# Row steps of the recurrence's block inverses on GpSimd, two to a place in the program, in a one-core decoder layer

## The chip, the cores and the metric

The kernel runs on one core of one Trainium2 chip. A time is the device time of one execution in microseconds (us). In profile rows PE is TensorE, PEld its weight loads, DVE VectorE, ACT ScalarE, POOL GpSimd and SP the engine that issues most DMAs.

## What is computed

One inference step of a decoder layer for 256 prompt tokens and 8 decoded ones: a SwiGLU FFN, a mixing stage (sliding-window attention beside an RWKV-7 recurrence with 16 heads of 64), and a second SwiGLU FFN. The change lies in the recurrence:

```python
def step(S, inp):
    r_t, lw_t, k_t, v_t, kk_t, a_t = inp
    sa = jnp.einsum('bhij,bhj->bhi', S, -kk_t)
    S = (S * jnp.exp(lw_t)[:, :, None, :] + sa[..., None] * (kk_t * a_t)[:, :, None, :]
         + v_t[..., None] * k_t[:, :, None, :])
    return S, jnp.einsum('bhij,bhj->bhi', S, r_t)
```

The kernel does not run these 256 steps one by one. It cuts the prompt into 4 chunks of 64 tokens. Within a chunk the effect of every token on later ones is a strictly triangular 64x64 matrix for each head, and the chunk needs the inverse of one minus it. That inverse is built from its two 32x32 diagonal blocks and one product that joins them.

## The kernel before, in words

**Stages.** All matmuls are fp32 work done as three products of split operands (`hi` and `lo`). `chunk` loads a piece of a weight of 128x512 into one of 6 buffers `raw` (SP), rounds it to `hi` (ACT, line 123) and subtracts `lo = raw - hi` (DVE, line 58), with 4 buffers each for `hi` and `lo`; `gemm` then issues 12 matmuls of 264 columns on it, into a PSUM tile `acc`. The first FFN ends at about 764 us, the mixing stage at about 1256 us, the second FFN fills the rest.

**The mixing stage** streams the input projection (38 tiles, `win`) and the output projection (three passes, `wout`) through `gemm`. All else is written as generators (`prep`, `chain`, `attend`, `dec_load`, `dec_attend`); after each `chunk` a `tick` moves each of them one `yield` further. `prep` runs for each of 8 pairs of heads, `chain` for each of 4 batches of two pairs. So a `yield` sets how many ticks a chain spans. The scheduler then reorders the instructions of each engine by a timeline of its own, and on the chip each engine works through its list strictly in that order.

**A chain.** `prep` multiplies out the triangular matrices `gm` and stores their diagonal blocks in a scratch tensor `sa` in DRAM. `chain` loads them twice: `X` holds a block on each of 32 partitions, copied four times (128 partitions), `Y` (called `Xt` in the profile) holds a quarter of its columns on each copy, 8 of 32. Then 30 row steps follow: step `s` multiplies (into `st`) and adds. `Y` goes to a second scratch tensor `sb` and comes back with other axes as `TT`; the unit diagonal is added there; `TN` is its transpose on DVE. Behind `TN` come the joining matmuls (`zs`), `kr`, `W`, `PT`, the products `N` and the steps over the 4 chunks (`Z`, `S`).

**Other names.** In `prep`, `wc`, `XD` and `t` are small tiles of the decode path; GpSimd copies to `XD`, then computes `t<-XD`, 16 columns that the matmul with the block matrix in `C` reads (PE's `m<-t,C`). `shc` are the last columns of each projected tile `pj`. `NSTEP` is the number of row steps for one `yield`, `DWAIT` the ticks that a chain waits after its loads, by batch.

Of the kernel before, what the change touches and what calls it, by code (L numbers as in the profile page):

```python
# [10 lines left out]
ALU = mybir.AluOpType  # L11
# [18 lines left out]
NS, NO, NY, NH, NT, NLD = 38, 8, 8, 40, 18, 6  # L30
NWARM = 14
NGM, NKR, NUV, NTT, NBT = 10, 5, 3, 2, 5
NSTEP = 4
DWAIT = (8,8,8,4)
PW = (2, 1, 3, 2, 2)
ALPHA = math.exp(-0.5)
LKV = 26
# [10 lines left out]
def body(tc, I, O):  # L48
    nc = tc.nc
    V, A, G, TE, SP = nc.vector, nc.scalar, nc.gpsimd, nc.tensor, nc.sync  # L50
# [6 lines left out]
    def tt(e, out, a, b, op):  # L57
        return e.tensor_tensor(out=out, in0=a, in1=b, op=op)  # L58
# [11 lines left out]
    def bc(ap, shape):  # L70
        return ap.broadcast_to(list(shape))
# [15 lines left out]
    def spawn(g):  # L87
        tasks.append(g)
        return g

    def pause(n):
        for _ in range(n):
            yield

    with ExitStack() as ctx:
# [7 lines left out]
        def slot(shape=(P, T), dt=F32, tag="s"):  # L103
            return sp.tile(list(shape), dt, tag=tag, bufs={"s": NS, "o": NO, "y": NY}[tag], name=uid(tag))

        def tmp(shape=(P, T), dt=F32):
            pool, n = cur[0]
            return pool.tile(list(shape), dt, tag="t", bufs=n, name=uid("t"))
# [223 lines left out]
        def mixing_body(mx, n2, n3, XD):  # L332
# [3 lines left out]
            def ring(shape, tag, bufs):  # L336
                return mx.tile(list(shape), F32, tag=tag, bufs=bufs, name=uid(tag))
# [6 lines left out]
            ident, bo, cm = C[:, CID:CID + P], C[:, CBO:CBO + P], C[:, CCM:CCM + P]  # L344
# [27 lines left out]
            def shifted(t, d):  # L372
                ps = win(t)
                pj = PJ[t % 3]
                with tc.high_priority():
                    tt(V, pj[:, 1:1 + T], ps[:, :T], rs, ALU.mult)
                G.tensor_copy(shc[:, t, :], pj[:, NP:NP + NB + 1])
                act(d[:, :NP], pj[:, 0:NP], AF.Copy, scale=vc(VMU + t))
                A.copy(d[:, NP:], ss[:, t, :])
                stt(d, pj[:, 1:1 + T], nmu[:, t:t + 1], d, ALU.mult, ALU.add)  # L380
                return d
# [133 lines left out]
            def chain(bt):  # L515
                n = bt.n
                while bt.left:
                    yield
                nr = n * 16
                ng = P // nr  # L520
                if ng == 3:
                    ng = 2
                nj = 32 // ng
                X = ring((ng * nr, 32, 32), "X", 1)
                Y = ring((ng * nr, nj, 32), "Xt", 1)
# [4 lines left out]
                TT = ring((P, n * 4, 64), "TT", NTT)  # L530
                for h in range(2):
                    G.memset(TT[h * 64 + 32:h * 64 + 64, :, 0:32], 0.0)
                yield from pause(DWAIT[bt.i])
                for s in range(1, 31):
                    m, w = -(-s // ng), 31 - s
                    t = ring((ng * nr, m, w), "st", 2)
                    shp = (ng * nr, m, w)
                    tt(V, t, bc(X[:, s:s + 1, s + 1:], shp), bc(Y[:, :m, s:s + 1], shp), ALU.mult)
                    tt(V, Y[:, :m, s + 1:], Y[:, :m, s + 1:], t, ALU.add)
                    if s % NSTEP == 0:  # L540
                        yield
                for g in range(ng):
                    SP.dma_start(scr2[bt.i].rearrange("r (j g t) -> g r j t", g=ng, t=32)[g], Y[g * nr:(g + 1) * nr])
                yield from pause(1)
                for h in range(2):
                    for blk in range(2):
                        x = h * 64 + blk * 32
                        SP.dma_start(TT[x:x + 32, :, blk * 32:blk * 32 + 32],
                                     scr2[bt.i].rearrange("(h b m) (s t) -> h b s m t", h=2, b=2, s=32)[h, blk])
                yield from pause(DWAIT[bt.i])  # L550
                for h in range(2):
                    for blk in range(2):
                        x = h * 64 + blk * 32
                        v = TT[x:x + 32, :, blk * 32:blk * 32 + 32]
                        tt(V, v, v, bc(ident[x:x + 32, x:x + 32].unsqueeze(1), (32, n * 4, 32)), ALU.add)
                TN = ring((P, n * 4, 32), "TN", 1)
                for h in range(2):
                    V.transpose(TN[h * 64:h * 64 + 32], TT[h * 64:h * 64 + 32, :, 0:32])
# [2 lines left out]
                for k in range(n):  # L561
                    for c in range(4):
                        for h in range(2):
                            j = k * 4 + c
# [26 lines left out]
                for k in range(n):  # L591
                    v = wus[k].rearrange("p (c t) -> p c t", c=4)
# [5 lines left out]
                for k in range(n):  # L598
                    for c in range(1, 4):
                        x = (c - 1) * P  # L600
# [6 lines left out]
                for k in range(n):  # L607
                    v = pbs[k][:, :384].rearrange("p (c t) -> p c t", c=3)
# [3 lines left out]
                for k in range(n):  # L612
                    for c in range(4):
                        x = (k * 4 + c) * 64
# [3 lines left out]
                for k in range(n):  # L618
                    for c in range(4):
                        x = (k * 4 + c) * 64  # L620
# [8 lines left out]
                for c in range(1, 4):  # L629
# [5 lines left out]
                    for k in range(n):  # L635
                        for h in range(2):
                            r = HALF[h]
                            x = (k * 4 + c) * 64
# [20 lines left out]
                for k in range(n):  # L659
                    p, o = bt.p0 + k, Ys[k]  # L660
# [169 lines left out]
            for kind, i in SEQ:  # L830
                if kind == "b":
                    bt = newbatch(i)
                    for k in range(BATCH[i]):
                        p = bt.p0 + k
                        x = [shifted(2 + 3 * p + j, tmp()) for j in range(3)]
                        spawn(prep(p, bt, k, *x))
                    bat.append(spawn(chain(bt)))
                    bts.append(bt)
                    if len(bat) == len(BATCH):
                        A.dma_start(O["sh"], shc)  # L840
                elif kind == "kv":
                    w, p = i // 2, i % 2
                    ps = win(LKV + i)
                    x = slot()
# [4 lines left out]
                else:  # L849
# [6 lines left out]
                    if i % 4 == 3:  # L856
                        p = i // 4
                        d = spawn(dec_attend(p, qs[4 * p:]))
# [183 lines left out]
```

## Time and profile before

| | |
|---|---|
| three runs | 2023.67, 2026.92, 2028.01 us, median 2026.92 |
| the profiled execution | 2027.84 us, of which 2026.1 us are the span of its instructions |
| PE busy | 1994.1 us (98%) |
| DVE, ACT, POOL busy | 1324.4, 1041.4 and 240.8 us |
| granted TensorE clock, mean | 0.994 |

A busy PE is not PE at its peak: matmuls overlap, and their ends are modelled. Rows of groups give the engine, the operation, out<-in, the count, busy us, mean ns of one, and the idle time before them with what ended it. Rows of a stretch give the busy time of each engine with its count of instructions, the granted clock, the share of the DMA engines and GB/s.

### The profile page before, as it was taken

The numbers are of one execution on the slowest core, as the hardware profiler recorded it, in microseconds if no ns is written. First come the engines' busy times: TensorE is split into PE (matmuls) and PEld (weight loads), VectorE is DVE, ScalarE is ACT, GpSimd is POOL, SyncE is SP. The second block draws the span as 40 slices with busy tenths as digits, with TensorE's granted clock in tenths as the row PEclk, the third lists the DMA queues.
The fourth block names the chain that finished last, engine by engine and source line by source line (L and its number), as shares of the span: only waits on it lengthen the run. The fifth ranks groups of instructions, "written<-read, shape, count | busy, mean of one in ns | idle before, by whom it ended". The sixth has DMA issues, their size and how long they took to land.

```text
span 2026.1 us, 45592 instructions
## 1 busy us (share of the span) xinstructions
PE 1994.1 (98%) x17126; PEld 1956.0 (97%) x17126; DVE 1324.4 (65%) x2674; ACT 1041.4 (51%) x2054; POOL 240.8 (12%) x342
## 2 busy tenths in 40 slices
PE   9999999999999999999999899999999999999998
PEld 9999999999999999998888789999999999999998
DVE  5865555655556577678778766775666666566665
ACT  5644444444444466665454555554444444444445
POOL 0401001010110122111110000120101101010012
PEclk9999999999999999999999999999999999999999
DMA  6565565655556566554456335565565555655654
GB/s 228 177 187 196 183 192 189 186 184 177 185 171 191 181 205 205 154 157 124 141 148 174 117 102 188 172 185 176 191 182 194 180 191 190 187 191 180 197 180 144
DMA packets 228798, 358.73 MB, mean 177 GB/s; under 512 B 42568, under 2 KB 83680, under 8 KB 228576
## 3 DMA queue, kind: packets, MB, share of 16 engines
q1 hardware_dynamic: 222112, 347.28, 54.6%
q10 hardware_dynamic: 6464, 8.54, 1.3%
q8 instruction: 134, 2.20, 0.4%
q14 instruction: 88, 0.72, 0.1%
HBM read 347.58 MB, written 10.22 MB: 177 GB/s over the span
## 4 chain that ended last, share of the span: by engine, by line
PE 94%; DVE 2%; DMA 2%; ACT 1%; SPq 1%; issue 1%; ACTq 0%; DVEq 0%
PE acc L74 85%; PE m L74 8%; DVE lo L58 1%; DMA TT<-sb 0%; DMA sb<-Xt 0%; DVE y L58 0%; DMA raw<-in_gu 0%; DMA ld<-in_sT 0%; DVE st L58 0%; SPq L122 0%; DVE Xt L58 0%; ACT t L68 0%; DVE uv L595 0%; DMA Xt<-sa 0%; PE m L495 0%
## 5 line engine op out<-in xcount | busy, mean ns | idle before, releaser
L58 DVE TENSOR_TENSOR lo<-raw,hi 128x512 fp32r<-128x512 f32 (+2 forms) x1304 | 871.8, 673 | 552.5 <-ACT hi L123 526.5
L123 ACT CAST hi<-raw 128x512 fp32r<-128x512 f32 (+2 forms) x1304 | 779.3, 602 | 861.6 <-PE acc L74 776.3
L74 PE MATMUL acc<-s,hi 128*128 128x264 f32 x5940 | 1107.3, 286 | 3.9 <-DVE s L58 1.6
L74 PEld LDWEIGHTS acc<-s,hi 128*128 128x128 f32 x5940 | 922.9, 188 | 10.0 <-ACT hi L123 2.2
L74 PE MATMUL acc<-s,lo 128*128 128x264 f32 x2970 | 848.3, 286 | 4.4 <-DVE lo L58 4.4
L74 PEld LDWEIGHTS acc<-s,lo 128*128 128x128 f32 x2970 | 559.5, 189 | 9.1 <-DVE lo L58 5.6
L74 PE MATMUL acc<-t,hi 128*128 128x264 f32 x2752 | 503.1, 284 | 0.0
L74 PEld LDWEIGHTS acc<-t,hi 128*128 128x128 f32 x2752 | 426.4, 188 | 0.0
L74 PE MATMUL acc<-t,lo 128*128 128x264 f32 x1376 | 389.0, 285 | 0.0
L58 POOL TENSOR_TENSOR t<-t,t 128x264 f32<-128x264 f32 (+1 forms) x148 | 150.7, 1018 | 1150.6 <-ACT hi L123 790.4
L74 PEld LDWEIGHTS acc<-t,lo 128*128 128x128 f32 x1376 | 258.4, 188 | 0.1
L74 PE MATMUL acc<-y,hi 128*128 128x264 f32 x648 | 124.5, 284 | 0.0
L74 PEld LDWEIGHTS acc<-y,hi 128*128 128x128 f32 x648 | 101.3, 188 | 0.2
L74 PE MATMUL acc<-y,lo 128*128 128x264 f32 x324 | 92.2, 285 | 0.0
L58 DVE TENSOR_TENSOR t<-acc,t 128x264 f32<-128x264 f32 x156 | 67.4, 432 | 36.8 <-PE acc L74 36.5
L58 POOL TENSOR_TENSOR o<-o,o 128x264 f32<-128x264 f32 x43 | 36.4, 846 | 222.7 <-ACT o L68 217.8
L74 PE MATMUL acc<-o,hi 128*128 128x264 f32 x324 | 62.8, 284 | 0.0
L74 PEld LDWEIGHTS acc<-y,lo 128*128 128x128 f32 x324 | 60.7, 187 | 0.0
L61 DVE SCALAR_TENSOR_TENSOR s<-acc,s 128x264 f32<-128x264 f32 x96 | 40.5, 427 | 16.0 <-PE acc L74 15.5
L74 PEld LDWEIGHTS acc<-o,hi 128*128 128x128 f32 x324 | 50.0, 188 | 0.0
L74 PE MATMUL m<-s,hi 128*128 128x264 f32 x260 | 48.5, 285 | 0.0
L61 DVE SCALAR_TENSOR_TENSOR x<-acc,x 128x264 f32<-128x264 f32 x96 | 40.5, 426 | 10.1 <-PE acc L74 9.6
(234 smaller groups left out, 1295.9 us busy)
## 6 DMA issues: line engine op xcount, KB each, us to landing
raw<-in_gu SPq DMA_DIRECT2D x688, 256.0 KB, 3.3
raw<-in_dn SPq DMA_DIRECT2D x224, 256.0 KB, 2.7
raw<-in_win SPq DMA_DIRECT2D x152, 256.0 KB, 3.5
raw<-in_dn SPq DMA_DIRECT2D x160, 192.0 KB, 2.7
raw<-in_wout SPq DMA_DIRECT2D x48, 256.0 KB, 3.3
raw<-in_wout SPq DMA_DIRECT2D x32, 128.0 KB, 2.9
xsp<-x ACTq DMA_DIRECT2D x16, 132.0 KB, 3.2
s<-xsp SPq DMA_DIRECT2D x16, 132.0 KB, 4.0
```

What stands on the lines that cost most here:

```text
L58: return e.tensor_tensor(out=out, in0=a, in1=b, op=op)
L61: return V.scalar_tensor_tensor(out=out, in0=a, scalar=s, in1=b, op0=op0, op1=op1)
L74: TE.matmul(out, lhsT, rhs, start=start, stop=stop, **k)
L123: A.copy(hi[:, :w], raw[:, :w])
```

## The change

The two instructions of each row step go from DVE to GpSimd. A `yield` comes after every second step in place of every fourth (15 in place of 7), and the last batch waits 8 ticks at both places, as the others do, in place of 4. The unit diagonal is no longer added by four DVE instructions in `TT`; GpSimd sets it by four strided fills in `Y`, before `Y` is stored.

```diff
-NSTEP = 4
-DWAIT = (8,8,8,4)
+NSTEP = 2
+DWAIT = (8, 8, 8, 8)
...
-                    tt(V, t, bc(X[:, s:s + 1, s + 1:], shp), bc(Y[:, :m, s:s + 1], shp), ALU.mult)
-                    tt(V, Y[:, :m, s + 1:], Y[:, :m, s + 1:], t, ALU.add)
+                    tt(G, t, bc(X[:, s:s + 1, s + 1:], shp), bc(Y[:, :m, s:s + 1], shp), ALU.mult)
+                    tt(G, Y[:, :m, s + 1:], Y[:, :m, s + 1:], t, ALU.add)
                     if s % NSTEP == 0:
                         yield
+                for g in range(ng):
+                    d = Y[g * nr:(g + 1) * nr].rearrange("p j t -> p (j t)")
+                    G.memset(d[:, g:nj * 32:32 + ng], 1.0)
...
                 yield from pause(DWAIT[bt.i])
-                for h in range(2):
-                    for blk in range(2):
-                        x = h * 64 + blk * 32
-                        v = TT[x:x + 32, :, blk * 32:blk * 32 + 32]
-                        tt(V, v, v, bc(ident[x:x + 32, x:x + 32].unsqueeze(1), (32, n * 4, 32)), ALU.add)
```

The scheduler places the chain anew. On DVE, before, the second batch's `TT` (here `TT_12573`, with its transpose `TN_13621`) stands among the weights' `lo` and the next pair's `kr`:

```order
L58 TENSOR_TENSOR lo_13983<-raw_13981,hi_13982 128x512
L411 RECIPROCAL t_13265<-m_13326 128x264
L61 TENSOR_SCALAR kr_13393<-t_13264,t_13332 128x256
L58 TENSOR_TENSOR kr_13393<-t_12581,t_13332 128x256
L58 TENSOR_TENSOR TT_12573<-TT_12573,C 32x8x32
L61 TENSOR_SCALAR t_13265<-t_13265,t_13264 128x264
L58 TENSOR_TENSOR lo_14016<-raw_14014,hi_14015 128x512
L58 TENSOR_TENSOR TT_12573<-TT_12573,C 32x8x32 x2
L558 STREAM_TRANSPOSE TN_13621<-TT_12573 32x256
```

Now, on DVE, the transpose of the second batch (`TN_13851`) stands here, between the first batch's `uv` and that batch's `kr`, `N`, `Z` and `S`:

```order
L58 TENSOR_TENSOR lo_13362<-raw_13360,hi_13361 128x512
L593 COPY uv_10754<-m_12958 64x4x64 x2
L593 COPY uv_10754<-m_12959 64x4x64 x2
L556 STREAM_TRANSPOSE TN_13851<-TT_12570 32x256
L58 TENSOR_TENSOR kr_11127<-m_13032,kr_11127 128x192
L556 STREAM_TRANSPOSE TN_13851<-TT_12570 32x256
L58 TENSOR_TENSOR kr_11492<-m_13033,kr_11492 128x192
L58 TENSOR_TENSOR N_12957<-m_13062,wc 128x512
L61 TENSOR_SCALAR Z_13138<-N_12957,wc 128x64 x2
L58 TENSOR_TENSOR lo_13396<-raw_13394,hi_13395 128x512
```

The second batch's transpose, with its wait for `TT`, has moved ahead of work that the first batch's chunk steps need.

On POOL, before, the third batch's first pair has its small instructions in a row up to `t<-XD`:

```order
L418 COPY wc<-t_12727 128x4
L58 TENSOR_TENSOR XD<-XD 128x8
L436 COPY XD<-t_12634 128x8
L436 COPY XD<-t_12630 128x8
L58 TENSOR_TENSOR t_12817<-XD 128x16
```

Now row steps of the second batch's chain (`X_12560`, `Xt_12561`) stand between them on POOL; these are the last of them ahead of the same `t<-XD`:

```order
L58 TENSOR_TENSOR st_13097<-X_12560,Xt_12561 128x66
L436 COPY XD<-t_12611 128x8
L58 TENSOR_TENSOR Xt_12561<-Xt_12561,st_13097 128x3x22
L58 TENSOR_TENSOR st_13100<-X_12560,Xt_12561 128x63
L58 TENSOR_TENSOR Xt_12561<-Xt_12561,st_13100 128x3x21
L58 TENSOR_TENSOR st_13144<-X_12560,Xt_12561 128x60
L58 TENSOR_TENSOR Xt_12561<-Xt_12561,st_13144 128x3x20
L436 COPY XD<-t_12607 128x8
L58 TENSOR_TENSOR st_13147<-X_12560,Xt_12561 128x57
L58 TENSOR_TENSOR t_12681<-XD 128x16
```

From the chain's first row step to this `t<-XD`, 23 row-step instructions now stand in POOL's list.

## The prediction

> **What bounds the kernel now.** I read the page's busy times and its chain, then stretches of the mixing stage, then single tiles and the timeline there.
>
> ```profile
> PE 1994.1 (98%) x17126; PEld 1956.0 (97%) x17126; DVE 1324.4 (65%) x2674; ACT 1041.4 (51%) x2054; POOL 240.8 (12%) x342
> PE 94%; DVE 2%; DMA 2%; ACT 1%; SPq 1%; issue 1%; ACTq 0%; DVEq 0%
> ```
>
> Of stretches the columns are: stretch, its length, busy us of PE, PEld, DVE, ACT and POOL with their counts, clock, DMA share, GB/s.
>
> ```profile
> 725.00:750.00 25.00, 25.00 (x208) 25.00 (x207) 21.14 (x40) 16.93 (x40) 6.37 (x8) 1.00 0.72 216
> 850.00:1110.00 260.00, 247.26 (x2642) 230.70 (x2641) 207.85 (x608) 144.52 (x339) 31.67 (x80) 0.99 0.52 149
> 900.00:925.00 25.00, 22.65 (x326) 21.16 (x325) 18.51 (x52) 12.13 (x27) 2.68 (x10) 0.93 0.47 128
> 1147.00:1175.00 28.00, 21.44 (x118) 15.81 (x117) 19.38 (x72) 16.49 (x52) 5.63 (x17) 0.76 0.19 63
> ```
>
> PE bounds it. DVE time that is freed pays only where PE stands idle: 260 - 247.3 = 12.7 us while the chains run (850 to 1110), and 28 - 21.4 = 6.6 us ahead of the second `wout` pass (1147 to 1175), where a clock of 0.76 costs another 0.24 x 28 = 6.7 us. So 26 us is all that can be won. The 900:925 row shows what a stand of 2.35 us costs beside itself: 0.07 x 25 = 1.75 us of lower clock.
>
> A matmul of `gemm` takes 25/208 = 0.12 us. For the small ones:
>
> ```profile
> L74 PE MATMUL acc<-s,hi 128*128 128x264 f32 x861 | 165.1, 289 | 1.0 <-DVE s L58 1.0
> L74 PE MATMUL acc<-s,lo 128*128 128x264 f32 x431 | 125.6, 293 | 4.4 <-DVE lo L58 4.4
> ```
>
> In the same 850 to 1110 us, 1292 large ones take 155 us, which leaves 92 us of busy time for 1350 small ones: 0.068 us each.
>
> **What the change removes.**
>
> ```profile
> L58 DVE TENSOR_TENSOR st<-X,Xt x120: 131/207/234, 851.6 to 1106.0; 128x60 f32<-128x60 f32 x16, 128x28 f32<-128x28 f32 x8, 128x48 f32<-128x48 f32 x8, 128x42 f32<-128x42 f32 x8
> L58 DVE TENSOR_TENSOR Xt<-Xt,st x120: 117/206/250, 851.8 to 1106.6; 128x60 f32<-128x60 f32 x16, 128x28 f32<-128x28 f32 x8, 128x48 f32<-128x48 f32 x8, 128x42 f32<-128x42 f32 x8
> L58 DVE TENSOR_TENSOR TT<-TT,C x16: 411/416/423, 898.5 to 1118.2; 32x256 f32<-32x256 f32 x16
> ```
>
> DVE loses 240 x 0.207 = 49.7 us of row steps and 16 x 0.416 = 6.7 us of diagonal adds. Nearly all of it lies beside a busy PE.
>
> **What a row step costs on POOL.** The trace of before has none there; the nearest rows are POOL's other two-input operations and its copies.
>
> ```profile
> L436 POOL COPY XD<-t x40: 183/266/1395, 785.8 to 1051.1; 128x8 f32<-128x8 f32 x40
> L58 POOL TENSOR_TENSOR XD<-XD x8: 198/205/206, 802.3 to 1039.7; 128x8 f32<-128x8 f32 x8
> L58 POOL TENSOR_TENSOR t<-XD x8: 223/692/1294, 808.2 to 1051.7; 128x16 f32<-128x16 f32 x8
> L436 POOL COPY XD<-t 128x8 f32<-128x8 f32 x40 | 16.7, 418 | 115.6 <-ACT t L68 41.3 <-DVE t L61 38.6 <-DVE t L58 35.7
> L58 POOL TENSOR_TENSOR t<-XD 128x16 f32<-128x16 f32 x8 | 5.6, 698 | 0.6
> L414 POOL MEMSET t<- 128x4 f32 x8 | 0.9, 107 | 0.0
> L58 POOL TENSOR_TENSOR s<-y,s 128x264 fp32r<-128x264 f32 x4 | 2.9, 744 | 41.3 <-PE m L74 40.0 <-ACT s L870 1.3
> 807.56 0.59 POOL L436 COPY XD<-t 128x8 f32<-128x8 f32 x1 [1.23 <-DVE t L61]
> 808.23 0.69 POOL L58 TENSOR_TENSOR t<-XD 128x16 f32<-128x16 f32 x1
> ```
>
> Undisturbed, 8 columns take 0.205 us, 16 take 0.223 and 264 take 0.744: 0.19 us and 2.1 ns a column. The loop bounds give a row step's instruction 47 columns on average, so 0.29 us. Each needs the one before it, and such a follower starts 0.08 us after the end (807.56 + 0.59 to 808.23): **0.37 us a row-step instruction, bare**.
>
> But the means lie far above the least values: 0.418 against 0.183 for the copies, 0.698 against 0.223 for `t<-XD`. The timeline shows why:
>
> ```profile
> 857.46 0.68 DVE L58 TENSOR_TENSOR lo<-raw,hi 128x512 fp32r<-128x512 f32 x1
> 857.51 0.69 POOL L436 COPY XD<-t 128x8 f32<-128x8 f32 x1 [2.00 <-DVE t L58]
> ```
>
> A copy of 8 columns, begun inside DVE's `lo`, ends 0.06 us after `lo` does. POOL waits out DVE's two-input instructions. The mean excess is 0.24 us (copies) to 0.48 us (`t<-XD`). I take 0.2, under the copies, as these POOL rows are released by DVE and meet its next instruction more often than a random start: **0.57 us an instruction while DVE works**, with 0.37 and 0.85 as ends.
>
> The Trainium skill, "SBUF — State Buffer", section "Who interferes with whom", says that a DVE instruction with two SBUF inputs and a GpSimd instruction that reads SBUF exclude each other, and the later one fully blocks. The pair above agrees (0.69 us in place of 0.19); by that rule DVE's `lo` also waits for row steps, so that part of the freed DVE time is paid back. The sum by the bare 0.37 us is 2047 us, by 0.57 us it is 2077 us (both below).
>
> **What waits for it.** DVE works in order, and the transpose `TN` waits for `TT`. From a batch's first row step to the place where DVE first needs `TT`, the program's lists hold these matmuls of PE (large + small), by 0.12 and 0.068 us:
>
> - before, batches 0 to 3: 282+89, 262+160, 243+154, 176+113, or 39.9, 42.3, 39.6, 28.8 us
> - after: 159+50, 118+117, 103+99, 120+114, or **22.5, 22.1, 19.1, 22.2 us**
>
> The scheduler has packed the chain into half the room. In this room POOL must do 60 row-step instructions, four fills (0.1 us each, by the fill of 4 columns above) and 10, 10, 8 and 2 other instructions (0.28 us bare with the gap). Then `Y` goes through DRAM:
>
> ```profile
> 891.60 1.95 DMA sb<-Xt
> 895.39 3.10 DMA TT<-sb
> 898.52 0.42 DVE TT L58
> L543 SPq DMA_DIRECT2D sb<-Xt x16: 555/600/713, 890.9 to 1108.7; - x16
> ```
>
> From the first issue (890.9) to DVE's start on `TT` (898.5) are 7.6 us, a round trip that the change keeps.
>
> Bare: 60 x 0.37 + 0.4 + 2.8 (2.8, 2.2, 0.6) + 7.6 = 33.0, 33.0, 32.4, 30.8 us, so DVE stands 10.5, 10.9, 13.3 and 8.6 us at `TN`, 43 us in all. At 0.57 us (0.48 for the others) until DVE stands, and bare from there: in batch 0, (22.5 - 4.8)/0.57 = 31 are done, 29 x 0.37 + 0.4 + 7.6 = 18.7 us are left; batches 1 to 3 likewise 19.0, 20.3 and 16.5, **74 us in all**. At 0.85 us (0.75 for others), 93 us.
>
> **What of it reaches PE.** While DVE stands, PE lives on the `hi` and `lo` already made.
>
> ```profile
> ACT hi L123 <- PE acc L74: 107.6, 109, 3.9
> ```
>
> ACT mostly waits for PE to free an `hi` (109 times in 760 to 1300 us), so all 4 buffers are usually full: 4 chunks of 12 matmuls, 5.8 us. That covers batches 0 and 3. In batches 1 and 2 DVE's row behind `TN` is the former batch's `kr` and `N`, which PE needs after 11 more large matmuls, 1.3 us. Together 14 us are covered, and another 4 us because PE's real pace holds 12.7 us of stands in 260. So PE stands 74 - 18 = 56 us longer (bare 25, upper 75). Part falls earlier: `t<-XD` sits behind 22 to 24 row-step instructions, and PE's `m<-t,C` waits for it; PE needs it after 72 to 78 large matmuls, about 9 us, while POOL needs 9 us bare and 14 us at 0.57 us, with some 2 us of others on top. The later stand at `TN` shrinks by as much, so I don't add it. SP also waits for POOL ahead of `sb<-Xt`, with loads of `raw` queued behind; its 6 buffers (8.7 us) cover most of that.
>
> **Gains.** In the new list the third batch's chain and the first decode attention come before the second `wout` pass, so I expect most of the 13.3 us at 1147 to 1175 back, say 10, and half of the 12.7 us, 6. **Clock**: six to eight stands by 1.75 us, but some in one window: 10 us. The Trainium skill, "TensorE: Matmul & The Clock Gate", Part 1, halves the clock after an idle window of about 3.4 us; the 0.93 above agrees in kind, and longer stands could cost more than I take.
>
> **Sum.** 2027.8 (the profiled execution) + 56 - 16 + 10 = 2078, less 0.9 since the median, 2026.9, lies that much lower: **2077 us**. Bare: 25 - 12 + 8 = +21, 2047 us. Upper: 75 - 10 + 15 = +80, 2107 us.
>
> **Rivals.**
>
> - *Bare POOL* (0.2): lock waits hardly matter, since PE's stands empty DVE: 2047 us. The excess in the rows of POOL speaks against it.
> - *Hidden chain, faster* (0.11): POOL ends in time, and DVE's relief fills PE's idle time: 2027 - 16 = 2011 us. It decides at `TN`: chain and round trip within 22 us need row-step instructions of (22.1 - 7.6 - 3.2)/60 = 0.19 us including gap and waits. A copy alone takes 0.183. For it speaks that PE takes up the first batch's `TN` late in the new list; against it, that DVE stands at `TN` whoever uses it.
> - *No change* (0.04): stands of 15 us cancel gains of 16: 2027 us.
> - *Chain worse* (0.1): 0.85 us an instruction, SP's queue starved of weights and long stretches at half clock: 2107 us and above.
>
> **How the numbers follow.** The forecast, stands at 0.57 us, has 0.55. The range leaves out the hidden chain and half of the worst case and takes the bare price: 2030 to 2107 us. About 0.2% (4 us) is what a measurement of this kernel can tell from no change: faster 0.11, same 0.04, slower 0.85.
>
> **What would show it.** Row-step rows on POOL at 0.35 to 0.6 us mean; waits of `DVE TN` for `DMA TT<-sb` of 30 us or more in total, in four pieces; `PE m` waiting for POOL `t` and for DVE `N`; POOL's chain from first `st` to `sb` over 25 us; PE idle in 850 to 1175 us well above the 20 us of now; little waiting in what is now 1147 to 1175. I am wrong if DVE's waits at `TN` stay near the present `TT` waits, or if PE's idle time shrinks.

## The result and the profile after

The changed kernel takes **2035.4 us** (median of 6, 2031.9 to 2040.0) against 2027.1 for the kernel before (6 runs): ratio 1.0043, 95% interval 1.0028 to 1.0058. It is slower, as forecast, but by 8 us and not by 50. The profiled execution took 2040.0 us, its span is 2038.2; that is 12.1 us longer than the span before, more than the 8 us between the medians, since the profiled execution is the slowest of its six.

From the page of the changed kernel, the busy times and the chain that ended last, by engine and by line:

```profile
PE 2000.8 (98%) x17126; PEld 1964.3 (96%) x17126; DVE 1288.7 (63%) x2418; ACT 1042.1 (51%) x2055; POOL 316.2 (16%) x598
PE 90%; POOL 4%; DMA 2%; issue 1%; DVE 1%; SPq 1%; ACT 1%; ACTq 0%; DVEq 0%; POOLq 0%
PE acc L74 82%; PE m L74 7%; POOL Xt L58 2%; POOL st L58 2%; DMA raw<-in_win 1%; DMA TT<-sb 1%; DMA raw<-in_gu 0%; DMA sb<-Xt 0%; ACT hi L123 0%; DVE lo L58 0%; DVE y L58 0%; SPq L546 0%; DVE t L675 0%; PE m L495 0%; ACT t L68 0%
```

DVE lost 36 us of busy time and POOL gained 75. (The prediction counted 56 us less on DVE. The lengths of its instructions sum to 50 us less, 1376 after 1427; in the records neighbours on DVE overlap, so that its busy time fell by less than that.) POOL, which was not in the chain of before, now holds 4% of it with the row steps (`Xt` and `st`, 2% each), and the transfer of `TT` stands behind them. PE's busy time rose by 6.7 us for the same work, at a lower clock (0.986 granted on average, 0.994 before).

Next the stretches. What changed in length is the mixing stage, 764 to 1256 us before and 765 to 1270 us after; outside it the spans agree to 1 us. First a row of the kernel before, then three of the changed one (columns as in the prediction):

```profile
764.00:1256.00 492.00, 472.10 (x4661) 436.35 (x4660) 369.37 (x1043) 283.06 (x684) 54.07 (x145) 0.98 0.50 149
```

```profile
765.00:1270.00 505.00, 479.63 (x4665) 445.34 (x4664) 334.63 (x787) 283.79 (x685) 128.70 (x402) 0.95 0.49 145
850.00:1110.00 260.00, 240.10 (x2494) 222.52 (x2493) 157.28 (x343) 137.75 (x334) 103.80 (x333) 0.93 0.46 127
1147.00:1175.00 28.00, 27.83 (x340) 24.08 (x342) 23.73 (x76) 18.01 (x56) 5.21 (x13) 1.00 0.46 143
```

PE idles 505 - 479.6 = 25.4 us in the stage, 5.5 more than before (492 - 472.1 = 19.9), and the same matmuls keep it busy 7.5 us longer, at a clock of 0.95 in place of 0.98. Together 13 us. While the chains run (850 to 1110) PE now idles 20 us in place of 12.7; the drain before the second `wout` pass (1147 to 1175), which had 6.6 us of idle time at a clock of 0.76, is gone.

Last, what PE waited for between 760 and 1300 us, in total, how often, and the longest, with DVE's wait at `TN` under it:

```profile
PE m L74 <- DVE N L58: 9.6, 2, 6.4
PE m L74 <- POOL t L58: 9.3, 3, 3.8
PE acc L74 <- DVE lo L58: 3.3, 2, 3.1
DVE TN L556 <- DMA TT<-sb: 29.0, 6, 10.5
```

These are the waits that the prediction named, at the places it named: `t<-XD` behind row steps in POOL's queue, `N` and `lo` behind `TN` in DVE's. They make 22.2 us of PE's 25.4. Of the other idle time only 3.2 us are left of 19.9, a gain of 16.7. So in this trace the change both won and lost, 17 against 22 us of idle time, and the lower clock added 7.5 us of busy time.

### The profile page after: what moved, and what is told of

Same layout as the page of the kernel before. It is cut to its first block, busy times and chain, and to the rows that moved or that the text cites. A ratio compares the mean times of both kernels' runs of the same rounds, so it can differ in the third digit from the quotient of the medians.

```text
span 2038.2 us, 45627 instructions
## 1 busy us (share of the span) xinstructions
PE 2000.8 (98%) x17126; PEld 1964.3 (96%) x17126; DVE 1288.7 (63%) x2418; ACT 1042.1 (51%) x2055; POOL 316.2 (16%) x598
## 4 chain that ended last, share of the span: by engine, by line
PE 90%; POOL 4%; DMA 2%; issue 1%; DVE 1%; SPq 1%; ACT 1%; ACTq 0%; DVEq 0%; POOLq 0%
PE acc L74 82%; PE m L74 7%; POOL Xt L58 2%; POOL st L58 2%; DMA raw<-in_win 1%; DMA TT<-sb 1%; DMA raw<-in_gu 0%; DMA sb<-Xt 0%; ACT hi L123 0%; DVE lo L58 0%; DVE y L58 0%; SPq L546 0%; DVE t L675 0%; PE m L495 0%; ACT t L68 0%
```

## The experiments

Theory A: time is lost only because POOL's chain with its round trip lasts longer than the place that the program gives it, so that instructions stand behind it in order. Rival B: row steps on POOL cost by themselves, since DVE and POOL hold each other up. Rival C: the new pacing (`NSTEP`, `DWAIT`) puts other work into worse places. After each edit the scheduler orders the instructions anew, so a run can differ in more than the lines named. "PE busy" is of the 325 us from 850 to 1175 in the run's trace; the last column is DVE's wait at `TN` (or `TT`, where the adds are kept) for the DMA. Work moves into and out of this stretch from kernel to kernel, so its busy time is a guide only: with the pacing alone it is lower than before, and the kernel faster.

| kernel | us | ratio to before, 95% | PE busy | DVE's wait |
|---|---|---|---|---|
| before | 2027 | 1 | 305.1 | 12.5 |
| changed | 2035.4 | 1.0043 (1.0028 to 1.0058) | 299.6 | 29.0 |
| pacing alone | 2023.3 | 0.9982 (0.9974 to 0.9991) | 302.1 | 13.1 |
| fills alone | 2018.0 | 0.9959 (0.9947 to 0.9971) | 309.7 | 12.3 |
| changed, old pacing | 2028.4 | 1.0008 (1.0000 to 1.0017) | 302.3 | 25.3 |
| changed, `TN` kept back | 2016.9 | 0.9951 (0.9938 to 0.9964) | 313.7 | 0 |
| changed, row steps on DVE | 2013.7 | 0.9932 (0.9918 to 0.9946) | 311.1 | 13.2 |
| the same, `TN` kept back | 2007.0 | 0.9896 (0.9883 to 0.9909) | 313.5 | 3.6 |
| changed, `XD` on DVE | 2043.3 | 1.0073 (1.0060 to 1.0086) | 284.2 | 50.9 |
| changed, `XD` on DVE, `TN` kept back | 2009.2 | 0.9914 (0.9902 to 0.9926) | 314.5 | 13.9 |
| `TN` kept back, two-input work added | 2027.0 | 0.9994 (0.9985 to 1.0003) | 305.0 | 4.9 |
| `TN` kept back, copies added | 2021.7 | 0.9979 (0.9967 to 0.9991) | 311.2 | 1.5 |
| before, `TN` kept back | 2028.4 | 1.0004 (0.9995 to 1.0013) | 303.9 | 13.4 |
| row steps of the last batch on POOL | 2004.6 | 0.9889 (0.9876 to 0.9903) | 317.7 | 1.7 |

### The parts of the change

**Pacing alone**, on the kernel before:

```diff
-NSTEP = 4
-DWAIT = (8,8,8,4)
+NSTEP = 2
+DWAIT = (8, 8, 8, 8)
```

> The kernel before with the new pacing alone (a place in the program every 2 row steps, 8 pauses in every batch); row steps and diagonal adds stay on VectorE. Theory A (the loss comes from chains that now end behind the instruction that needs them: POOL's t<-XD, and N and lo behind TN): a row step on VectorE takes 0.2 us and ends long before it is needed, so nothing stands: 2024 to 2032 us. Theory C (the new pacing alone moves other work into worse places): about 2035 us, as long as the changed kernel.

It gains 0.18%. With the row steps on DVE, C falls: the pacing does no harm there. In its trace PE does not idle from 1147 to 1175 us, where the kernel before had 6.6 us of idle time and the changed kernel 0.2:

```profile
1147.00:1175.00 28.00, 28.00 (x378) 25.25 (x376) 21.87 (x81) 14.17 (x41) 0.00 (x0) 1.00 0.21 63
```

**Fills alone**, on the kernel before:

```diff
+                for g in range(ng):
+                    d = Y[g * nr:(g + 1) * nr].rearrange("p j t -> p (j t)")
+                    G.memset(d[:, g:nj * 32:32 + ng], 1.0)
...
-                        tt(V, v, v, bc(ident[x:x + 32, x:x + 32].unsqueeze(1), (32, n * 4, 32)), ALU.add)
```

> The kernel before with the diagonal alone changed: strided fills on POOL ahead of the stores in place of the 16 adds on VectorE; row steps stay on VectorE, old pacing. VectorE loses 16 x 0.416 = 6.7 us of adds and four waits for TT stay. Theory A: 2020 to 2027 us; theory C the same; if POOL's fills in the chain cost more than the adds did, 2028 us and above.

It gains 0.41%, the largest gain of the three parts, for 16 memsets of 0.1 us in place of 16 adds of 0.416. The 8.7 us are more than the 6.7 us of the adds, and DVE's wait at `TN` is as long as before; where the gain arises was not followed.

**The changed kernel with the row steps back on DVE**:

```diff
-                    tt(G, t, bc(X[:, s:s + 1, s + 1:], shp), bc(Y[:, :m, s:s + 1], shp), ALU.mult)
-                    tt(G, Y[:, :m, s + 1:], Y[:, :m, s + 1:], t, ALU.add)
+                    tt(V, t, bc(X[:, s:s + 1, s + 1:], shp), bc(Y[:, :m, s:s + 1], shp), ALU.mult)
+                    tt(V, Y[:, :m, s + 1:], Y[:, :m, s + 1:], t, ALU.add)
```

> The changed kernel with the row steps alone put back on VectorE; new pacing and POOL's fills stay. Theory A (what costs is only that POOL's chain outlasts the room the lists give it): no stand for t<-XD, N or lo, and the gains of pacing (3.3 us) and fills (8.7 us) add up: 2012 to 2018 us. Theory B (row steps on GpSimd also cost by themselves, through VectorE's and GpSimd's instructions in each other's way): clearly under the changed kernel with TN kept back (2016.9), by more than 4 us.

Pacing and fills add up (0.9982 x 0.9959 = 0.9941; measured 0.9932). So under the new pacing the move to POOL costs 1.0043/0.9932, 1.1% or 22 us, of which the gains of the other two parts paid 14.

**The changed kernel with the old pacing**:

```diff
-NSTEP = 2
-DWAIT = (8, 8, 8, 8)
+NSTEP = 4
+DWAIT = (8,8,8,4)
```

> The changed kernel with the old pacing (a place every 4 row steps, pauses 8, 8, 8, 4). The program's lists give a chain about 22 us from its first row step to TN here too (22.5, 21.5, 21.9, 22.6). Theory A: POOL still needs 26 us and the round trip 7, so TN stands again, some 25 to 35 us in all, and PE waits for N, lo and t<-XD: 2030 to 2042 us. Theory C: as before, about 2027 us.

The time came out 2 us under A's range, but the stand at `TN` is the expected one, and in this order PE meets it at `gm` and `lo`; for POOL's `t` it waits once in place of three times:

```profile
PE m L74 <- DVE gm L58: 12.4, 2, 7.7
PE m L74 <- POOL t L58: 3.8, 1, 3.8
PE acc L74 <- DVE lo L58: 3.7, 1, 3.7
DVE TN L556 <- DMA TT<-sb: 25.3, 4, 10.8
```

The time itself says more. With the row steps on POOL the old pacing is 7 us faster than the new one (1.0008 against 1.0043, with intervals that do not touch), while with the row steps on DVE the new one is the faster. So C falls only for row steps on DVE. And the price of the move depends on the pacing: 0.5% or 10 us under the old one (1.0008/0.9959, both with the fills), 22 us under the new one. Under the old pacing next to nothing is lost against the kernel before.

### Taking the waits away

**`TN` kept back**: the changed kernel, with one line pinned to its place in the program text.

```diff
-                    V.transpose(TN[h * 64:h * 64 + 32], TT[h * 64:h * 64 + 32, :, 0:32])
+                    tc.keep_in_program_order(V.transpose(TN[h * 64:h * 64 + 32], TT[h * 64:h * 64 + 32, :, 0:32]))
```

> The changed kernel with the two transposes TN kept at the place where the program text has them, which moves them far back in VectorE's list (from the first row step of a batch, some 190 to 296 large matmuls of PE lie ahead of TN in place of 103 to 159); nothing else is changed. Theory A: VectorE's wait at TN falls from 29 us to under 3, PE's waits for N (9.6 us) and lo (3.3) go, that for POOL's t<-XD (9.3 us) stays, and the clock rises with it: 2015 to 2024 us. Theory B (GpSimd and VectorE slow each other's two-input instructions, wherever TN stands): 2033 to 2038 us, and the row steps' mean rises above 0.34 us as VectorE no longer stands beside them.

This is the deciding run. The row steps stay on POOL and last as long as before (0.350 us on average in place of 0.339, 26 to 28 us a chain), and 18 us go. PE's waits in its trace, between 760 and 1270 us, are down to these:

```profile
PE m L74 <- POOL t L58: 10.5, 3, 4.8
PE m L74 <- ACT bk L804: 0.6, 1, 0.6
PE acc L74 <- POOL s L58: 0.2, 1, 0.2
```

`N` and `lo` are gone with DVE's stand, and `t` stays, as A said. B's rise of the row steps is there, but it is 0.01 us each.

**`XD` on DVE**: the changed kernel, with what stood behind the row steps in POOL's queue moved to DVE.

```diff
-                    G.tensor_copy(XD[:, i, p, :], src[:, NP:T])
+                    V.tensor_copy(XD[:, i, p, :], src[:, NP:T])
...
-                tt(G, XD[:, 7, p, :], XD[:, 1, p, :], XD[:, 5, p, :], ALU.mult)
-                tt(G, dq, XD[:, 2:5:2, p, :], bc(XD[:, 5:6, p, :], (P, 2, NB)), ALU.mult)
+                tt(V, XD[:, 7, p, :], XD[:, 1, p, :], XD[:, 5, p, :], ALU.mult)
+                tt(V, dq, XD[:, 2:5:2, p, :], bc(XD[:, 5:6, p, :], (P, 2, NB)), ALU.mult)
```

> The changed kernel with POOL's copies into XD and its two products of them (XD<-XD and t<-XD) on VectorE; row steps stay on POOL. Theory A: PE's wait for POOL's t (9.3 us) goes with the lower clock behind it (3 us), VectorE pays 56 small instructions of some 0.1 us, mostly beside a busy PE; the stands at TN (29 us) stay: 2020 to 2028 us. If the wait for t were only the same stand met earlier, TN's stand would grow by as much and the time would stay at 2033 to 2037 us.

A's number was wrong by 15 us, and its alternative was right in direction: PE's wait for `t` is gone, and the stand at `TN` grew by more than that wait.

```profile
PE m L74 <- DVE uv L593: 26.1, 2, 13.1
PE acc L74 <- DVE lo L58: 10.9, 3, 5.4
DVE TN L556 <- DMA TT<-sb: 50.9, 6, 15.2
```

In both kernels `TN` starts 33.0 to 34.6 us after its batch's first row step. But DVE gets there after 33.9, 26.2, 24.7 and 23.8 us in the changed kernel, and after 25.1, 19.3, 18.7 and 23.1 us here: PE is not held up for `t` on the way, and in batches 1 and 2 the new order has fewer small matmuls ahead of `TN`. PE needs `uv`, which is queued behind it. Of 50.9 us at `TN` 37 reach PE, of the changed kernel's 29.0 it was 12.9: about 15 us are covered in both.

**Both**: `TN` kept back and `XD` on DVE.

> Both of it: the changed kernel with TN kept back and with the XD copies and products on VectorE. Theory A: both waits gone, none of the chain's work stands in front of another: 2016.9 - 10.5 (PE's wait for POOL's t there) - 1 to 3 of clock = 2003 to 2007 us. Theory B: 2012 us or more, since VectorE, busy beside all row steps, then slows them and itself: row steps over 0.36 us mean.

The two waits go together: 2009.2 us. That is 2 us above A's range and 3 under B's. In the fourth batch the program puts `TN` only 116 large matmuls after the first row step, and there 10.7 us of stand are back (13.9 in all). The row steps rose to 0.364 us, as B has it, without the time following.

**Row steps on DVE and `TN` kept back**: both edits above that name `tt(V` and `keep_in_program_order`.

> The changed kernel with the row steps back on VectorE and the transposes TN kept at the place of the program text. Theory A: with the row steps on VectorE TN has room already (164 to 300 large matmuls), so that keeping it back gains little: within 4 us of the same kernel without it. If more than 4 us are gained, the waits for TT that the kernel before had (12.5 us) matter too, and part of the gain of keeping TN back was never due to GpSimd.

It gains 6.7 us more, beyond the 4 of A: DVE's waits for `TT` (13.2 us, 3.6 left) did matter. So of the 18 us that the pin gained on the changed kernel, some 7 are had with the row steps on DVE as well, and the other 11 or 12 belong to POOL. This kernel is also the measure for B: with both waits taken away, row steps on POOL (and `XD` on DVE) take 2009.2 us, row steps on DVE 2007.0, and the intervals of the two overlap. That leaves little for a cost of POOL's row steps by themselves.

**The kernel before with `TN` and the adds kept back**:

```diff
-                        tt(V, v, v, bc(ident[x:x + 32, x:x + 32].unsqueeze(1), (32, n * 4, 32)), ALU.add)
+                        tc.keep_in_program_order(tt(V, v, v, bc(ident[x:x + 32, x:x + 32].unsqueeze(1), (32, n * 4, 32)), ALU.add))
...
-                    V.transpose(TN[h * 64:h * 64 + 32], TT[h * 64:h * 64 + 32, :, 0:32])
+                    tc.keep_in_program_order(V.transpose(TN[h * 64:h * 64 + 32], TT[h * 64:h * 64 + 32, :, 0:32]))
```

> The kernel before, with the diagonal adds and the transposes TN kept at the place of the program text, and nothing of the change. With the row steps on VectorE keeping TN back gained 6.7 us (2013.7 to 2007.0) beside the new pacing and the fills. If that gain is a matter of TN's place alone, the kernel before gains it too: 2017 to 2023 us. If it needs the fills or the pacing, 2024 to 2029.

No gain: in this program the pin hardly moves anything (282, 259, 243 and 176 large matmuls lie between a batch's first row step and the adds; without it 282, 262, 243 and 176), and DVE's wait at `TT` stays (13.4 us). In these runs the pin paid only where it moved the instruction away from its DMA.

### What DVE costs a row step

The changed kernel with `TN` kept back, and one more DVE instruction at every place of a chain. **Two SBUF inputs**:

```diff
+        dump = cp.tile([P, 320], mybir.dt.bfloat16, name="dump")
...
                     if s % NSTEP == 0:
+                        tc.keep_in_program_order(tt(V, dump, C[:, 0:320], C[:, 320:640], ALU.add))
                         yield
```

> Measures the disputed term, what VectorE's work costs a row step on POOL. The changed kernel with TN kept back, and at each place of a chain one more VectorE instruction with two SBUF inputs (320 columns, an addition of constants, kept in program order; its output is not used), 15 a batch. Without it a chain's 60 row-step instructions last 3.4 us longer than 0.19 us + 2.1 ns a column gives (0.057 us each), beside 19 to 22 VectorE instructions with two SBUF inputs (9 to 13 us). If the wait goes by the number of VectorE's instructions, each of which can hold up one row step by half its own length on average, 15 more of about 0.45 us bring 3 us more a chain: 0.09 to 0.12 us each. If the excess has nothing to do with VectorE it stays at 0.05 to 0.06. If each row step waits whenever VectorE works (the price of 0.2 us of the prediction), it comes to 0.2. VectorE's time rises by 25 us beside a busy PE: 2016 to 2030 us.

**One input**, as the control:

```diff
+                        tc.keep_in_program_order(V.tensor_copy(dump, C[:, 0:320]))
```

> As the kernel with the additional two-input instructions, but with a VectorE copy of 320 columns (one SBUF input) at the same places, as the control for mere work on VectorE. If only two-input instructions hold POOL up, the excess of a row step stays at 0.05 to 0.06 us; if any VectorE instruction does, it rises in proportion to the copy's length: 0.07 to 0.09. 2014 to 2025 us.

The added instructions ran as planned in the first batch only; in the others most of them fell outside the chain. There the two-input kernel has 36 DVE instructions with two SBUF inputs beside the 60 row-step instructions in place of 22, and the row steps' excess over 0.19 us + 2.1 ns a column is 6.2 us in place of 3.3: 0.103 us each, as forecast from the number of DVE's instructions, and half of the prediction's 0.2. With 10 more copies in that batch it is 4.2 us, 0.070 us each, which was the forecast for the case that any DVE instruction holds POOL up; but a chain without copies has 4.5 us in the kernel with `TN` kept back, so 1 us in one chain does not settle whether a copy costs anything. Over all 29 chains of eight kernels (15 to 36 such DVE instructions a chain) the excess is 0.10 to 0.21 us for each of DVE's instructions, 0.17 on average. **So the cost goes by DVE's instructions**, and is not a fixed price for each of POOL's 60: it is as if one DVE instruction held up at most one row step, and the next one started free behind it. Chains with more of these DVE instructions also have more of their time (the two rise together, and the excess follows each equally well), so whether the number or the length counts is open.

### The last batch alone on POOL

The fastest kernel of the runs above, with

```diff
-                    tt(V, t, bc(X[:, s:s + 1, s + 1:], shp), bc(Y[:, :m, s:s + 1], shp), ALU.mult)
+                    tt(G if bt.i == 3 else V, t, bc(X[:, s:s + 1, s + 1:], shp), bc(Y[:, :m, s:s + 1], shp), ALU.mult)
```

and the addition after it likewise.

> The fastest kernel so far (row steps on VectorE, POOL's fills, new pacing, TN kept back: 2007.0 us) with the row steps of the last batch alone on POOL, where 2 other POOL instructions stand among them in place of 10 and TN comes 170 large matmuls after the first row step. If a POOL chain that has room and holds up nobody is free, and VectorE's 12 us of row steps there lie beside a busy PE: 2004 to 2009 us. If the row steps on POOL cost by themselves, 2010 us or more.

2004.6 us, the fastest of all, 1.1% under the kernel before (the step from 2007.0 is within the two intervals). PE is busy 317.7 of the 325 us, at full clock:

```profile
850.00:1175.00 325.00, 317.72 (x3445) 290.17 (x3444) 261.27 (x778) 194.85 (x498) 62.71 (x172) 1.00 0.51 146
```

## Why the prediction was right and wrong

**Right: the mechanism.** The order of who waits for whom was right, and the pin showed it. The round trip through DRAM, put at 7.6 us, took 5.7 to 8.9 us from the first issue of `sb` to `TN`. Gains and clock together were put at -16 + 10 = -6 us and are -16.7 + 7.5 = -9.2 us. Term by term the two cannot be compared, since the 16 us hold clock regained at 1147 to 1175 us, and the 7.5 us are what is left after it. The part of DVE's stand that PE does not feel was put at 18 us and is 16, partly by luck: it was to be 5.8 us in batches 0 and 3, 1.3 in batches 1 and 2 and 4 on top; it was the whole stand of 1.5 us in batch 0, and 3.7, 3.5 and 7.7 us in the others.

**Wrong: DVE's stand at `TN`, 74 us forecast, 29 measured**, and with it PE's, 56 us forecast, 22 measured. That term alone is 34 of the 42 us between forecast and result; 3 more are gains and clock, and 5 lie between the profiled execution, by which these terms go, and the median. Two of its factors failed.

*The price of a row step.* The step that put 0.2 us of waiting on each instruction was wrong. On the changed kernel's row steps:

```profile
L58 POOL TENSOR_TENSOR Xt<-Xt,st 128x60 f32<-128x60 f32 (+10 forms) x120 | 41.1, 343 | 8.4
L58 POOL TENSOR_TENSOR st<-X,Xt 128x60 f32<-128x60 f32 (+10 forms) x120 | 40.3, 336 | 20.9 <-DMA raw<-in_win 6.8 <-DMA ld<-in_sT 4.9 <-DMA Xt<-sa 1.3
L58 POOL TENSOR_TENSOR st<-X,Xt x120: 207/294/822, 852.6 to 1101.9; 128x60 f32<-128x60 f32 x16, 128x28 f32<-128x28 f32 x8, 128x48 f32<-128x48 f32 x8, 128x42 f32<-128x42 f32 x8
```

The bare 0.29 us stands in the median (0.294). The mean, 0.339, is 0.05 us above it: in a chain 8 to 12 of 60 instructions are held up by more than 0.1 us. With the gap of 0.08 us that is 0.42 us in place of 0.57, and a chain runs 25.3 to 27.2 us from first to last row step. The prediction took the wait from POOL's copies, most of which are started by DVE's own results; 20 of the 40 took over 0.1 us more than the least, one in two, against one in six of the row steps. It said that they meet DVE's next instruction more often, and still discounted that too little. The Trainium skill, "SBUF — State Buffer", section "Who interferes with whom", has the later instruction fully blocked. That agrees: the longest row step is 0.822 us, and `lo` beside row steps takes 0.726 us on average (38 of them) against 0.690 elsewhere in the mixing stage. How often it happens in a back-to-back chain is what the prediction got wrong.

*The room.* The rooms of 22.5, 22.1, 19.1 and 22.2 us were too short, in part by an error of counting. The number of small matmuls came from the program's list; their price of 0.068 us came from the trace's records. These are not the same units:

```profile
L74 PE MATMUL m<-TN,gm x128: 191/191/257, 924.6 to 1160.3; 32*32 32x32 f32 x128
```

The loops around this `mm` make 4 batches x 2 x 4 x 2 = 64 calls, and the trace has 128 records: most small matmuls, with their f32 operands, leave two. (The whole program lists 16115 matmuls; the trace has 17126.) The list's 50, 117, 99 and 114 small ones are 90, 228, 193 and 222 records, and the rooms are 159 x 0.12 + 90 x 0.068 = 25.2 us, and likewise 29.7, 25.5 and 29.5.

These are not the measured rooms either. DVE reached `TN` 26.2, 24.7 and 23.8 us after the first row step in batches 1 to 3; in batch 0 after 33.9 us, as PE was held up by `t` before, and after 25.1 us in the kernel with `XD` on DVE, where it was not. So the recount fits batches 0 and 2 and is 3.5 and 5.7 us too long in batches 1 and 3; why was not followed.

With the measured rooms (25.1, 26.2, 24.7 and 23.8 us) the prediction's own rule at 0.57 us gives 65 us of stand in place of 74. With the measured chains and round trips too (33.8, 32.9, 34.0 and 34.2 us together) it gives 8.7 + 6.7 + 9.3 + 10.4 = 35 us. 29.0 were measured (1.5, 6.9, 9.9 and 10.7): the last 6 are batch 0's, where the wait for `t` came first. So the rule holds, and its inputs failed: about 9 us by the room, 30 by the price.

*Smaller.* `t<-XD` was not added, as its stand was to be taken off that at `TN`. Batch 0 bears this out: with `XD` on DVE its stand at `TN` is 8.5 us in place of 1.5. Of PE's 22 us, 9.3 stand at `t` and 12.9 behind `TN`. The bare sum comes to 2048 by its own terms, not 2047. Two of the signs that the prediction named came out just short: row steps of 0.339 us where 0.35 to 0.6 were named, and 29.0 us at `TN`, nearly all in three pieces, where 30 or more in four were named.

**The rivals.** In the time "No change" was nearest, 8 us off, but with 15 us of stands where PE had 22. In its terms "Bare POOL" was nearest: PE's stand was put at 25 us, and waits between DVE and POOL do hardly matter. Its reason for that, that PE's stands empty DVE, is not the one: with `TN` kept back DVE does not stand, and the row steps take 0.350 us. With its 43 us at `TN` it too had the rooms too short. "Hidden chain, faster" failed at `TN`, where it said it would be decided; with `TN` kept back the kernel is faster, at 2016.9 us, though PE still waits 10.5 us for `t`.

## What to carry to other kernels

An instruction moved to a slower engine is paid for at the first instruction that stands, in order, in front of other work and waits for it: look where the program puts that instruction, and move it back before judging the engine (one pinned line was worth 18 us here, more than the whole change had cost). A change in several parts is measured part by part, and in pairs: the fills and the pacing alone gained 0.4% and 0.2%, the move they came with ate both, and beside that move the pacing lost 0.35%. When a length of time is worked out from a program's list and a trace's mean, count both in the same unit.

## What was not expected of the hardware

POOL and DVE shared the work better than the rows of before suggested: with 60 dependent POOL instructions beside some 20 DVE instructions with two SBUF inputs, a chain lost 2.5 to 4.5 us in the kernels without added work and with `XD` on POOL. And a stand of PE costs more than itself: with `TN` kept back the span of the profiled execution fell by 27 us (the slowest run of the one kernel against the fastest of the other, 18 us by the medians), of which 13.6 are PE's idle time and 13.6 its busy time. In the traces' record of the granted clock the mixing stage has only the values 1 and 0.5, and the stretches at 0.5 last 3.41 us or a multiple of it. The changed kernel spends 47.8 us at half clock there, the kernel before and the one with `TN` kept back 20.5 us each, and the fastest kernel none. Half of PE's busy time in these stretches, as an estimate of what they cost, is 21 us in the changed kernel and 9 in each of the two others. The prediction took 1.75 us of clock for a stand, which is what one stretch of 3.41 us costs; three of the changed kernel's six stretches are 10.24 us long. In the mean the clock is 0.95 in the stage of the changed kernel against 0.98 with `TN` kept back:

```profile
760.00:1270.00 510.00, 498.69 (x4924) 466.91 (x4923) 356.51 (x823) 303.31 (x721) 133.41 (x404) 0.98 0.53 156
```
